# The end of a one-core transformer step, taken by stream: gates by slot, sums of squares by products with ones, the last two experts added apart

## The chip, the core and the metric

One core of a Trainium2 chip runs the whole program. TensorE (PE in the profile, its weight loads PEld) multiplies into PSUM banks; VectorE (DVE), ScalarE (ACT) and GpSimd (POOL) work elementwise; SyncE (SP) issues the transfers. The metric is the device time of one execution in microseconds (us), the median of the runs. Less is better.

## The reference, cut to what matters

Two streams of 128 tokens (prompt and sample, 256 token columns in all) go through one layer: a mixer, then a mixture of 32 experts of which each token takes four, then a final norm. Only the end bears on this change:

```python
def expert_step(acc, e):
    w_gu_e, b_gu_e, w_down_e, b_down_e, w_tok = e
    g, u = jnp.split(t @ w_gu_e + b_gu_e, 2, axis=-1)
    g = jnp.minimum(g, SWIGLU_LIMIT)
    u = jnp.clip(u, -SWIGLU_LIMIT, SWIGLU_LIMIT)
    act = (u + 1.0) * g * jax.nn.sigmoid(SWIGLU_ALPHA * g)
    out = act @ w_down_e + b_down_e
    return acc + w_tok[:, None] * out, None
...
x = x + g2 * _moe(h, lp)        # g2: one gate per channel and stream
...
y = x * rsqrt(mean(x * x) + EPS) * norm_final
```

## The kernel before, in words

The residual `xT` lies transposed: 128 partitions of channels, eight tiles (`k` 0 to 7) of 256 token columns, the first 128 of them one stream and the rest the other. Each expert's weights come in six transfers of 2 MB (four for gate and up, `w_gu`; two for down, `w_dn`) into eleven places that are used in turn (`load_unit`, line 389, issue on line 402); SP issues them in one queue, well ahead of their use.

An expert (`expert`) works on up to 64 tokens that chose it, its slots. `up` calls `expert_up`: 64 matmul records for gate and up (line 1233; each fp32 product stands as two records), in the order in which the four pieces land, then four short bias products (line 1238). `expert_act` does the activation on VectorE and ScalarE (lines 1246 to 1250): clip the gate half, tanh on ScalarE, clip the up half, two multiplications. `down` of the expert before turns the activation round (`transposed`, line 1285, copied on line 1288) and multiplies it by the down weights (line 1298); `keep_y` copies the result. Experts are added in pairs: `scatter_pair` builds the matrix that spreads slots back to tokens (lines 1257 to 1272, tile `sT`), and `add_out` (line 1313) spreads and adds into `xT` through `add_gated` (line 1177), which multiplies by the channel's gate `fin[:, s, k]`. An even expert has slots 0 to 63 in channel tiles 0 to 3 and slots 64 to 127 in tiles 4 to 7; an odd one has the other halves.

TensorE's order in an expert is written by hand (`manual_schedule`); the other engines' instructions are ordered by the scheduler. For the last expert, 31, the order is: `bias_products` (the down biases by the routing weights), down of expert 30, `scatter_pair(30)`, up of 31, its activation, and `add_out(bias, "pa", ...)`, the bias term added to `xT`. PSUM banks are named by tags: C has two, A has three, B, D and E one each.

`finale` (line 1467) then runs alone: down of expert 31; per quarter `c`, the copy of its result beside expert 30's, the spreading products (line 1480), the gated adds into `xT`, squares on ScalarE (line 1483) and the norm weight on ScalarE or GpSimd (lines 1487, 1489); GpSimd adds three squares together (line 1493); column sums by products with one column of ones (line 207); GpSimd's power for 1/sqrt on 128x2 (line 193); TensorE spreads it over the partitions (line 201); VectorE multiplies (lines 1509, 1513) and five transfers write `o_tokens` (line 1514).

Of the kernel before, what the change touches and what calls it, by code (L numbers as in the profile page):

```python
# [20 lines left out]
P = 128  # L21
# [42 lines left out]
def hybrid_step(ctx, tc, A):  # L64
# [324 lines left out]
    def load_unit(u, h):  # L389
# [11 lines left out]
        for i in range(0, k, step):  # L401
            npc_ins[0] = nc.sync.dma_start(t[:, i:i + step], src[:, i:i + step])
# [781 lines left out]
    def bias_products():  # L1184
# [8 lines left out]
        cbT = place(6 * NE % NUNIT, "cbT", 0)[:, 0:2 * P].rearrange("e (s t) -> e s t", s=2)  # L1193
# [26 lines left out]
    def expert_up(e, xg, w, banks, m, after=None, half_way=None):  # L1220
# [5 lines left out]
        for k in range(KC):  # L1226
            if half_way and k == KC // 2 - 1:
                half_way()
            with tc.issue_after(after.ins) if after else ExitStack():
                for i in range(2):  # L1230
                    for q in range(nq):
                        c0 = i * D + part[q] * wd
                        PE.matmul(banks[i][m * q:m * q + m, 0:wd], xg[:, k, :], w[k][:, c0:c0 + wd],  # L1233
                                  start=(k == 0), stop=False, skip_group_check=True)
        for i in range(2):
            for q in range(nq):
                c0 = i * D + part[q] * wd
                PE.matmul(banks[i][m * q:m * q + m, 0:wd], sel3[:, e:e + 1].to_broadcast([96, m]), b3[:, c0:c0 + wd],
                          start=False, stop=True, skip_group_check=True)
        return banks  # L1240

    def expert_act(banks, name, m, tag="gm"):
# [4 lines left out]
        S.activation(tg, gm, AF.Tanh, scale=0.851)  # L1247
        V.tensor_scalar(um, banks[1][:, 0:wd], 7.0, -7.0, op0=ALU.min, op1=ALU.max)
        V.scalar_tensor_tensor(gm, tg, 1.0, gm, op0=ALU.add, op1=ALU.mult)
        V.scalar_tensor_tensor(gm, um, 1.0, gm, op0=ALU.add, op1=ALU.mult)  # L1250
        return gm

# [55 lines left out]
    def add_out(products, name, tags="CCCC"):  # L1308

        for j in range(0, KC, 2):  # L1310
            pc = bank(tags[j // 2], f"{name}pc{j}", 3 if tags[j // 2] == "A" else 2)
# [3 lines left out]
        return ins  # L1315

# [96 lines left out]
    def up(e):  # L1413
        return expert_up(e, xgs.pop(e), w, up_banks(e, f"e{e}pgu"), CAP, last,
                         (lambda: gather_first(0, (1,)), lambda: down(0))[e] if e < 2 else None)
# [4 lines left out]
    def expert(e):  # L1420
# [13 lines left out]
        if e == NE - 1:  # L1434
            bias = bias_products()
        if e > 1:
            last = down(e - 1)
            if e % 2:
                scatter_pair(e - 1)

# [7 lines left out]
        acts[e] = (expert_act(banks, f"e{e}", CAP), w)  # L1448
# [6 lines left out]
        else:  # L1455

            add_out(bias, "pa", ("C", "C", "A", "A"))
# [9 lines left out]
    def finale():  # L1467
        down(NE - 1)
        y, py = ys[NE - 2], last_y[0]
        pss = bank("E", "pssl", 1)  # L1470
        products = pair_products(sT[NE - 2], y)
        sq = place((6 * NE + 1) % NUNIT, "sql", 0)[:, 0:2 * D].rearrange("p (k t) -> p k t", t=T)

        def finish(c):

            cs = slice(c * P, (c + 1) * P)
            keep_y(y, py, 1, cs)
            pc = bank("C", f"pcl{c}", 2)
            for i, k in enumerate((c, c + 4)):
                PE.matmul(pc[:, i * T:(i + 1) * T], *products[k], start=True, stop=True)  # L1480
            add_tiles_gated((c, c + 4), pc)
            for k in (c, c + 4):
                S.activation(sq[:, k], xT[:, k], AF.Square)
            if c < 3:
                for k in (c, c + 4):
                    if c < 2:
                        S.activation(xT[:, k], xT[:, k], AF.Copy, scale=fin[:, 2, k:k + 1])
                    else:
# [110 lines left out]
```

## Time and profile before

| | us |
|---|---|
| median of 3 runs | 1434.85 |
| lowest, highest | 1432.95, 1436.88 |
| the profiled execution | 1435.31 |
| its span | 1433.5 |

Over the span PE is busy for 1339.8 us (93%), DVE for 590.3, ACT for 335.9 and POOL for 104.2; HBM is read at 352 GB/s on the mean, and in the stretch of the experts at some 424 GB/s. [...] In a timeline row the numbers are the start in the span, the time from the first start to the last end of the merged instructions, and in brackets the idle time before them with what ended it.

### The profile page before, as it was taken

What the parts mean: (1) busy time and instruction counts of PE and PEld (TensorE: products, weight loads), DVE (VectorE), ACT (ScalarE), POOL (GpSimd) and SP (SyncE); (2) the same over time, 40 slices, a digit from 0 to 9 for tenths busy, and PEclk for the clock granted to TensorE, in tenths of its full rate; (3) what the DMA queues carried; (4) which work ended last, traced back from release to release, by engine and by line L of the source; (5) the groups of instructions that cost most, each with busy time, mean ns of one, the idle gap of its engine ahead of it and who ended that gap; (6) DMA issues with size and microseconds to landing.
All of it is one profiled execution on the core that took longest, in us unless ns stands there. A gap on an engine that the chain in (4) does not pass through costs nothing. (4 is left out here: it accounts for less than half of the span.)

```text
span 1433.5 us, 20977 instructions
## 1 busy us (share of the span) xinstructions
PE 1339.8 (93%) x8577; PEld 793.9 (55%) x8577; DVE 590.3 (41%) x1270; ACT 335.9 (23%) x631; POOL 104.2 (7%) x118
## 2 busy tenths in 40 slices
PE   7999999999999999999999899999999999898885
PEld 3988989898999643443443344344344343333332
DVE  4856879898776322132132222213213212212124
ACT  2534656575664110010000000001001000000001
POOL 1112313431002000000000000000000000000001
PEclk8999999999999999999999999999999999999997
DMA  9997566556877899999999999999999999999981
GB/s 360 294 278 203 186 231 235 215 181 224 318 284 263 333 406 424 423 426 423 423 427 424 410 423 425 424 426 423 425 424 426 424 424 425 425 425 424 426 337 35
DMA packets 83710, 506.53 MB, mean 353 GB/s; under 512 B 6866, under 2 KB 34130, under 8 KB 51410
## 3 DMA queue, kind: packets, MB, share of 16 engines
q1 hardware_dynamic: 80658, 497.71, 87.1%
q10 hardware_dynamic: 2880, 6.60, 1.3%
q8 instruction: 99, 1.62, 0.5%
q14 instruction: 73, 0.60, 0.1%
HBM read 498.26 MB, written 5.64 MB: 352 GB/s over the span
## 5 line engine op out<-in xcount | busy, mean ns | idle before, releaser
L303 DVE TENSOR_TENSOR wl<-win,wh 128x1024 fp32r<-128x1024 f32 (+1 forms) x84 | 100.7, 1211 | 36.0 <-ACT wh L302 24.7
L302 ACT CAST wh<-win 128x1024 fp32r<-128x1024 f32 (+1 forms) x84 | 84.0, 1010 | 73.4 <-PE pbc L330 19.2
L1493 POOL TENSOR_TENSOR sql<-sql 128x256 f32<-128x256 f32 x3 | 2.2, 727 | 944.9 <-PE pcl L1480 944.6
L714 POOL TENSOR_TENSOR m<-m_half,adt 128x512 fp32r<-128x512 f32 x32 | 42.5, 1347 | 87.1 <-PE pss L717 87.1
L330 PE MATMUL pxs<-hT,wh 128*128 128x256 f32 x256 | 37.5, 291 | 0.0
L330 PE MATMUL pgt<-hT,wh 128*128 128x256 f32 x256 | 36.0, 287 | 1.0 <-ACT wh L302 1.0
L330 PE MATMUL pz<-hT,wh 128*128 128x256 f32 x256 | 36.7, 288 | 0.0
L330 PE MATMUL pbc<-hT,wh 128*128 128x256 f32 x256 | 35.6, 287 | 0.0
L330 PEld LDWEIGHTS pxs<-hT,wh 128*128 128x128 f32 x256 | 32.5, 190 | 3.6 <-issue 2.8
L330 PE MATMUL pso<-yhl,wh 128*128 128x256 f32 x256 | 34.1, 284 | 0.0
L330 PEld LDWEIGHTS pgt<-hT,wh 128*128 128x128 f32 x256 | 32.4, 191 | 3.0 <-issue 1.9
L330 PEld LDWEIGHTS pz<-hT,wh 128*128 128x128 f32 x256 | 32.5, 190 | 1.5 <-issue 1.5
L330 PEld LDWEIGHTS pbc<-hT,wh 128*128 128x128 f32 x256 | 32.2, 190 | 1.9 <-issue 1.7
L330 PEld LDWEIGHTS pso<-yhl,wh 128*128 128x128 f32 x256 | 32.1, 192 | 0.0
L330 PE MATMUL pglu<-hT,wh 128*128 128x256 f32 x192 | 27.1, 292 | 0.0
L330 PEld LDWEIGHTS pglu<-hT,wh 128*128 128x128 f32 x192 | 25.1, 199 | 0.7 <-issue 0.7
L303 DVE TENSOR_TENSOR wl<-wso,wh 128x1024 fp32r<-128x1024 f32 x16 | 19.5, 1223 | 7.5 <-ACT wh L302 7.3
L697 ACT ACTIVATE gd<-gm,dtT 128x128 f32<-128x128 f32 x64 | 20.8, 415 | 4.4 <-DVE gm L688 4.3
L698 DVE SCALAR_TENSOR_TENSOR gd<-gm,dtT,gd 128x128 f32<-128x128 f32 x64 | 21.0, 377 | 1.6 <-ACT gd L697 1.2
L302 ACT CAST wh<-wso 128x1024 fp32r<-128x1024 f32 x16 | 16.7, 1046 | 14.3 <-PE pso L330 10.8
L330 PE MATMUL pwo<-mhl,wh 128*128 128x256 f32 x128 | 18.9, 290 | 0.3 <-DVE mhl L1008 0.3
L1233 PE MATMUL e26pgu<-w,xg 128*64 128x512 f32 x64 | 16.1, 654 | 3.2 <-DMA w<-in_w_gu 2.9
(1095 smaller groups left out, 2632.8 us busy)
## 6 DMA issues: line engine op xcount, KB each, us to landing
w<-in_w_gu SPq DMA_DIRECT2D x116, 2048.0 KB, 30.4
w<-in_w_down SPq DMA_DIRECT2D x57, 2048.0 KB, 26.3
win<-in_w_in_pack SPq DMA_DIRECT2D x38, 1024.0 KB, 6.5
ada<-in_w_ada SPq DMA_DIRECT2D x10, 1024.0 KB, 9.1
wso<-in_w_ssd_out SPq DMA_DIRECT2D x8, 1024.0 KB, 6.0
im<-dru SPq DMA_DIRECT2D x16, 312.0 KB, 8.5
wcf<-in_w_conf_out SPq DMA_DIRECT2D x4, 1024.0 KB, 8.8
wo<-in_w_o SPq DMA_DIRECT2D x4, 1024.0 KB, 9.7
```

Of the source, the lines that this page charges most:

```text
L302: S.copy(hi[:, ks, 0:m], w[:, ks])
L303: V.tensor_tensor(lo[:, ks, 0:m], w[:, ks], hi[:, ks, 0:m], ALU.subtract)
L330: last_wo[0] = PE.matmul(out, w[:, k, 0:n], m[:, k, :], start=first and i == 0, stop=last and i == len(order) - 1, skip_group_check=True)
L697: S.activation(gd[s][:, h, :], gm[:, 0, s, :], AF.Copy, scale=dtT[:, 0, s, c0:c0 + 1])
L698: V.scalar_tensor_tensor(gd[s][:, h, :], gm[:, 1, s, :], dtT[:, 0, s, 32 + c0:33 + c0], gd[s][:, h, :], op0=ALU.mult, op1=ALU.add)
L714: G.tensor_tensor(m4[d], m_half[:, d, None, None, :].to_broadcast([P, 2, 4, 64]), ac[d], ALU.mult)
L1233: PE.matmul(banks[i][m * q:m * q + m, 0:wd], xg[:, k, :], w[k][:, c0:c0 + wd], start=(k == 0), stop=False, skip_group_check=True)
L1493: G.tensor_tensor(sq[:, 0], sq[:, 0], sq[:, k], ALU.add)
```

## The change

It touches the last expert and what follows it, and one transfer.

- The transfer of piece 1 of expert 28 is issued as three, of 112, 7 and 9 rows.
- `expert_up` of expert 31 multiplies its last two row tiles for the gate half first, adds the gate's bias, and then does the up half. `expert_act` does its first multiplication before it clips the up half.
- Before expert 31's up products, TensorE writes the gates as rows (`gates_by_slot`: 16 transposes of a broadcast column into banks C, copied to SBUF by ScalarE in four halves).
- Expert 30's share is no longer added with expert 31's. `add_two` adds the bias term and expert 30's slots together, for four channel tiles before expert 31's up products and for the other four after its activation.
- The end: VectorE multiplies expert 31's down result by the gates, once per stream, out of PSUM; TensorE spreads it (half of the partitions for each product, 128 columns of one stream); VectorE adds `xT`; ScalarE squares; products of a 128x128 block of ones with the squares give the sums already spread over the partitions; the norm weight, the scale and the power (GpSimd, now on 128x128 for each stream) follow; four transfers write the output, by stream and half of the channels.

```diff
--- before.py
+++ after.py
@@ -399,7 +399,8 @@
         step = k // 2 if e == NE - 1 and c > 3 else k
         for i in range(0, k, step):
-            npc_ins[0] = nc.sync.dma_start(t[:, i:i + step], src[:, i:i + step])
+            for r in (slice(0, 112), slice(112, 119), slice(119, P)) if (e, c) == (28, 1) else (slice(0, P),):
+                npc_ins[0] = nc.sync.dma_start(t[r, i:i + step], src[r, i:i + step])
         return [t[:, i] for i in range(k)]
     def parts(u):
@@ -1181,7 +1182,7 @@
             for s in range(2):
                 add_gated(k, s, pc[:, i * T + s * P:i * T + (s + 1) * P])
-    def bias_products():
+    def bias_products(spare):
         b_dn = con.tile([P, D // 4], F32, name="b_dn", tag="g1_0")
         S.dma_start(b_dn, A["b_down_pack"])
@@ -1190,7 +1191,7 @@
             for s in range(2):
                 PE.matmul(pct[q * NE:(q + 1) * NE, s * P:(s + 1) * P], comb[:, s], ident, start=True, stop=True,
                           skip_group_check=True)
-        cbT = place(6 * NE % NUNIT, "cbT", 0)[:, 0:2 * P].rearrange("e (s t) -> e s t", s=2)
+        cbT = spare[:, 0:2 * P].rearrange("e (s t) -> e s t", s=2)
         V.tensor_copy(cbT, pct[:, 0:2 * P].rearrange("e (s t) -> e s t", s=2))
         rows = [slice(k // 2 * NE, (k // 2 + 1) * NE) for k in range(KC)]
         return [(b_dn[r, k % 2 * P:(k % 2 + 1) * P], cbT[r]) for k, r in enumerate(rows)]
@@ -1217,38 +1218,52 @@
     def over_banks(name, n):
         return [bank(t, f"{name}{i}", b) for i, (t, b) in enumerate((("D", 1), ("C", 2), ("C", 2), ("E", 1))[0:n])]
-    def expert_up(e, xg, w, banks, m, after=None, half_way=None):
+    def expert_up(e, xg, w, banks, m, after=None, half_way=None, gate_first=False):
         nq = P // m
         wd = D // nq
         part = (0, 1) if nq == 2 else (0, 2, 1, 3)
-        for k in range(KC):
+        def rows(k, i):
+            for q in range(nq):
+                c0 = i * D + part[q] * wd
+                PE.matmul(banks[i][m * q:m * q + m, 0:wd], xg[:, k, :], w[k][:, c0:c0 + wd],
+                          start=(k == 0), stop=False, skip_group_check=True)
+        def bias(i):
+            for q in range(nq):
+                c0 = i * D + part[q] * wd
+                PE.matmul(banks[i][m * q:m * q + m, 0:wd], sel3[:, e:e + 1].to_broadcast([96, m]), b3[:, c0:c0 + wd],
+                          start=False, stop=True, skip_group_check=True)
+        together = KC - 2 if gate_first else KC
+        for k in range(together):
             if half_way and k == KC // 2 - 1:
                 half_way()
             with tc.issue_after(after.ins) if after else ExitStack():
                 for i in range(2):
-                    for q in range(nq):
-                        c0 = i * D + part[q] * wd
-                        PE.matmul(banks[i][m * q:m * q + m, 0:wd], xg[:, k, :], w[k][:, c0:c0 + wd],
-                                  start=(k == 0), stop=False, skip_group_check=True)
+                    rows(k, i)
         for i in range(2):
-            for q in range(nq):
-                c0 = i * D + part[q] * wd
-                PE.matmul(banks[i][m * q:m * q + m, 0:wd], sel3[:, e:e + 1].to_broadcast([96, m]), b3[:, c0:c0 + wd],
-                          start=False, stop=True, skip_group_check=True)
+            for k in range(together, KC):
+                rows(k, i)
+            bias(i)
         return banks
-    def expert_act(banks, name, m, tag="gm"):
+    def expert_act(banks, name, m, tag="gm", gate_first=False):
         wd = D * m // P
         gm = sm.tile([P, wd], F32, name=name + "gm", tag=tag, bufs=1)
         tg, um = (sm.tile([P, 512], F32, name=name + n, tag=t, bufs=1)[:, 0:wd] for n, t in (("tg", "aT"), ("um", "um")))
         V.tensor_scalar(gm, banks[0][:, 0:wd], 7.0, None, op0=ALU.min)
         S.activation(tg, gm, AF.Tanh, scale=0.851)
+        if gate_first:
+            V.scalar_tensor_tensor(gm, tg, 1.0, gm, op0=ALU.add, op1=ALU.mult)
         V.tensor_scalar(um, banks[1][:, 0:wd], 7.0, -7.0, op0=ALU.min, op1=ALU.max)
-        V.scalar_tensor_tensor(gm, tg, 1.0, gm, op0=ALU.add, op1=ALU.mult)
-        V.scalar_tensor_tensor(gm, um, 1.0, gm, op0=ALU.add, op1=ALU.mult)
+        if not gate_first:
+            V.scalar_tensor_tensor(gm, tg, 1.0, gm, op0=ALU.add, op1=ALU.mult)
+        last_act_ins[0] = V.scalar_tensor_tensor(gm, um, 1.0, gm, op0=ALU.add, op1=ALU.mult)
         return gm
+    last_act_ins = [None]
     def slots_of(out, e, poss):
@@ -1305,14 +1320,25 @@
             r = slice(CAP * q, CAP * (q + 1))
             (V.tensor_copy if q else S.copy)(ys[q ^ swap][r, cols], py[r, cols])
-    def add_out(products, name, tags="CCCC"):
+    def add_out(products, name):
         for j in range(0, KC, 2):
-            pc = bank(tags[j // 2], f"{name}pc{j}", 3 if tags[j // 2] == "A" else 2)
+            pc = bank("C", f"{name}pc{j}", 2)
             for i in range(2):
                 ins = PE.matmul(pc[:, i * T:(i + 1) * T], *products[j + i], start=True, stop=True)
             add_tiles_gated((j, j + 1), pc)
         return ins
+    def add_two(one, two, c, tag, bufs, after=None):
+        pcs = [bank(tag, f"papc{c}{h}", bufs) for h in range(2)]
+        for x in (one, two):
+            for i in range(2):
+                for h in range(2):
+                    PE.matmul(pcs[h][:, i * T:(i + 1) * T], *x[c + i + 4 * h], start=x is one and i == 0, stop=x is two, skip_group_check=True)
+        with tc.issue_after(after.ins) if after else ExitStack():
+            for h in range(2):
+                add_tiles_gated((c + 4 * h, c + 4 * h + 1), pcs[h])
     def pair_products(sT, ys):
         return [(ys[k // 4][:, k % 4 * P:(k % 4 + 1) * P], sT[:, k // 4]) for k in range(KC)]
@@ -1412,7 +1438,7 @@
     def up(e):
         return expert_up(e, xgs.pop(e), w, up_banks(e, f"e{e}pgu"), CAP, last,
-                         (lambda: gather_first(0, (1,)), lambda: down(0))[e] if e < 2 else None)
+                         (lambda: gather_first(0, (1,)), lambda: down(0))[e] if e < 2 else None, e == NE - 1)
     def add_pair(e):
         return add_out(pair_products(sT[e], ys[e]), f"e{e}")
@@ -1432,11 +1458,17 @@
                 combine()
         if e == NE - 1:
-            bias = bias_products()
+            spare = place(6 * NE % NUNIT, "spare", 0)
+            bias = bias_products(spare)
         if e > 1:
             last = down(e - 1)
             if e % 2:
                 scatter_pair(e - 1)
+            if e == NE - 1:
+                gates_by_slot(spare)
+                first = [(ys[e - 1][k // 4][own(0, k // 4), k % 4 * P:(k % 4 + 1) * P], sT[e - 1][own(0, k // 4), k // 4]) for k in range(KC)]
+                add_two(bias, first, 0, "C", 2)
             load_pieces(6 * e + NUNIT)
         overflow(e, w, more)
@@ -1445,7 +1477,7 @@
             gather_first(1)
         if e == 1:
             scatter_pair(e - 1)
-        acts[e] = (expert_act(banks, f"e{e}", CAP), w)
+        acts[e] = (expert_act(banks, f"e{e}", CAP, gate_first=e == NE - 1), w)
         if e % 2 == 0:
             if e:
@@ -1454,7 +1486,24 @@
             gather_slots(e + 1)
         else:
-            add_out(bias, "pa", ("C", "C", "A", "A"))
+            add_two(bias, first, 2, "A", 3, last_act_ins[0])
+    def own(i, h):
+        return slice(CAP, P) if i ^ h else slice(0, CAP)
+    gslot = []
+    def gates_by_slot(spare):
+        for s in range(2):
+            t = spare[:, 512 + 512 * s:1024 + 512 * s]
+            for h in range(2):
+                pt = bank("C", f"pgs{s}{h}", 2)
+                for k in range(4):
+                    PE.transpose(pt[:, k * P:(k + 1) * P], fin[:, s, 4 * h + k:4 * h + k + 1].to_broadcast([P, P]), ident)
+                S.copy(t[own(1, h)], pt[own(1, h)])
+            gslot.append(t)
     w = last = mores = None
     last_y = []
@@ -1466,52 +1515,48 @@
     def finale():
         down(NE - 1)
-        y, py = ys[NE - 2], last_y[0]
-        pss = bank("E", "pssl", 1)
...
-        for k in (0, 2, 6, 3, 7):
-        rf = rstd_of(pss[:, 0:2], 1.0 / D, EPS, "rf")
-        bcast_rows(rbf, rf)
...
+        py = last_y[0]
+        sl = sT[NE - 2]
+        t = place((6 * NE + 1) % NUNIT, "fin1", 0)
+        yg = [t[:, 512 * s:512 * s + 512] for s in range(2)]
+        xs, sq = {}, {}
+        places = (t[:, 2 * D:], place((6 * NE + 2) % NUNIT, "fin2", 0))
+        for s in range(2):
+            for h in range(2):
+                xs[s, h], sq[s, h] = (places[s][:, (2 * i + h) * 512:(2 * i + h + 1) * 512].rearrange("p (k t) -> p k t", t=P) for i in range(2))
+        for s in range(2):
+            V.tensor_tensor(yg[s], py, gslot[s], ALU.mult)
+        pcs = {}
+        for s in range(2):
+            pc = [bank("CA"[s], f"pcl{s}{h}", 3 if s else 2) for h in range(2)]
+            for k in range(4):
+                for h in range(2):
+                    r = own(1, h)
+                    PE.matmul(pc[h][:, k * P:(k + 1) * P], yg[s][r, k * P:(k + 1) * P], sl[r, h, s], start=True, stop=True,
+                              skip_group_check=True)
+            for h in range(2):
+                pcs[s, h] = pc[h].rearrange("p (k t) -> p k t", t=P)
+        ss = bank("E", "ssl", 1)
+        for s in range(2):
+            for h in range(2):
+                V.tensor_tensor(xs[s, h], pcs[s, h], xT[:, 4 * h:4 * h + 4, s * P:(s + 1) * P], ALU.add)
+                S.activation(sq[s, h], xs[s, h], AF.Square)
+        for s in range(2):
+            for h in range(2):
+                for k in range(4):
+                    PE.matmul(ss[:, s * P:(s + 1) * P], one.to_broadcast([P, P]), sq[s, h][:, k],
+                              start=(h == 0 and k == 0), stop=(h == 1 and k == 3), skip_group_check=True)
+        for s in range(2):
+            for h in range(2):
+                V.tensor_tensor(xs[s, h], xs[s, h], fin[:, 2, 4 * h:4 * h + 4].unsqueeze(2).to_broadcast([P, 4, P]), ALU.mult)
+            v = yg[0][:, s * P:(s + 1) * P]
+            V.tensor_scalar(v, ss[:, s * P:(s + 1) * P], 1.0 / D, EPS, op0=ALU.mult, op1=ALU.add)
+            G.tensor_tensor(v, v, mhalf[:, 0:1].to_broadcast([P, P]), ALU.pow)
+            for h in range(2):
+                V.tensor_tensor(xs[s, h], xs[s, h], v.unsqueeze(1).to_broadcast([P, 4, P]), ALU.mult)
+                nc.sync.dma_start(A["o_tokens"][512 * h:512 * h + 512, s * P:(s + 1) * P].rearrange("(k p) t -> p k t", p=P), xs[s, h])
     with tc.manual_schedule(engines={mybir.EngineType.PE}):
         finale()
```

## Rows read from the trace of the kernel before

**Rows 1.** The windows view, last expert to last down products; its columns head it.

```profile
core 0: us, PE busy (x) PEld busy (x) DVE busy (x) ACT busy (x) POOL busy (x), PEclk, DMA share, GB/s
...
1396.00:1400.00 4.00, 3.73 (x20) 1.29 (x20) 0.00 (x0) 0.00 (x0) 0.00 (x0) 1.00 0.06 27
1400.00:1404.00 4.00, 1.46 (x20) 0.76 (x16) 3.81 (x11) 0.63 (x1) 0.00 (x0) 1.00 0.06 27
1404.00:1408.00 4.00, 1.85 (x6) 1.03 (x8) 2.89 (x10) 0.59 (x1) 0.00 (x0) 0.50 0.02 10
1408.00:1412.00 4.00, 4.00 (x14) 1.20 (x12) 0.00 (x0) 0.00 (x0) 0.00 (x0) 0.64 0.00 0
```

**Rows 2.** The chain that ended last: start us, length us, what.

```profile
1396.27 3.65 PE e31pgu L1233 x16
...
1401.47 1.11 DVE xT L1177 x4
...
1403.18 1.55 DVE xT L1177 x6
...
1407.25 8.88 PE e31py L1298 x32
...
1429.44 0.39 DVE xT L1509
```

**Rows 3.** Timeline, TensorE and ScalarE around the last expert's gate and up products.

```profile
1383.23 0.66 PE L1269 MATMUL pst<-ident,sg 128*128 128x128 f32 x4
...
1383.92 0.59 ACT L1272 COPY sT<-pst 128x512 f32<-128x512 f32 x1
...
1384.04 1.94 PE L1233 MATMUL e31pgu<-w_0a,xg 128*64 128x512 f32 x8
...
1391.39 3.65 PE L1233 MATMUL e31pgu<-w,xg 128*64 128x512 f32 x16 [0.27 <-DMA w<-in_w_gu]
...
1396.27 3.65 PE L1233 MATMUL e31pgu<-w,xg 128*64 128x512 f32 x16 [1.23 <-DMA w<-in_w_gu]
...
1399.76 0.60 PE L1238 MATMUL e31pgu<-b,sel 96*64 96x512 bf16 x4
```

**Rows 4.** Timeline, TensorE groups that price the new and moved products.

```profile
1351.99 7.09 PE L1233 MATMUL e30pgu<-w,xg 128*64 128x512 f32 x32 [0.29 <-PEq L1343]
...
1369.81 1.99 PE L1313 MATMUL e28pc<-sT,y 128*128 128x256 f32 x8
...
1374.83 0.71 PE L1285 MATMUL e30pat<-ident,e30gm 128*128 128x128 f32 x4
...
1376.21 7.09 PE L1298 MATMUL e30py<-w,e30aT 128*64 128x512 f32 x32 [0.68 <-ACT e30aT L1288]
...
1400.29 1.17 PE L1313 MATMUL papc<-cbT,b_dn 32*128 32x256 f32 x16
```

**Rows 5.** Timeline, first steps of the last expert's activation.

```profile
1400.18 0.69 DVE L1246 TENSOR_SCALAR e31gm<-e31pgu 128x512 f32<-128x512 f32 x1 [15.53 <-PE e31pgu L1238]
...
1400.79 0.68 DVE L1248 TENSOR_SCALAR e31um<-e31pgu 128x512 f32<-128x512 f32 x1
...
1400.97 0.63 ACT L1247 ACTIVATE e31tg<-e31gm 128x512 f32<-128x512 f32 x1 [16.46 <-DVE e31gm L1246]
```

**Rows 6.** Prices for the new end: timeline, then groups by line and form.

```profile
1422.57 2.70 PE L207 MATMUL pssl<-one,sql 128*128 128x1 f32 x20 [0.71 <-POOL sql L1493]
...
L854 DVE TENSOR_TENSOR modr<-modr,pm 128x512 f32<-128x512 f32 x6 | 4.1, 684 | 1.1 <-PE pm L226 1.0
...
L767 ACT ACTIVATE ysq<-y 128x512 f32<-128x512 f32 x8 | 5.0, 625 | 3.1 <-DVE y L765 3.1
```

**Rows 7.** GpSimd's groups by line and form: busy us, mean ns, idle before.

```profile
L734 POOL TENSOR_TENSOR le<-L,dtT 128x4 f32<-128x4 f32 x16 | 6.3, 418 | 10.1 <-ACT L L721 10.1
...
L1493 POOL TENSOR_TENSOR sql<-sql 128x256 f32<-128x256 f32 x3 | 2.2, 727 | 944.9 <-PE pcl L1480 944.6 <-ACT sql L1483 0.3
...
L193 POOL TENSOR_TENSOR rf<-rfv,mhalf 128x2 f32<-128x2 f32 x1 | 0.7, 719 | 1.2 <-DVE rfv L191 1.2
```

More of the change, by code (lines that the diff above doesn't have):

```diff
@@ L1468, in finale @@
         down(NE - 1)
-        y, py = ys[NE - 2], last_y[0]
-        pss = bank("E", "pssl", 1)
[L1471 to L1488, printed above, removed]
-                        G.tensor_scalar(xT[:, k], xT[:, k], fin[:, 2, k:k + 1], None, op0=ALU.mult)
@@ L1491, in add_squares @@
-        def add_squares(*ks):
-            for k in ks:
-                G.tensor_tensor(sq[:, 0], sq[:, 0], sq[:, k], ALU.add)
-        finish(0)
-        add_squares(4)
-        finish(1)
-        add_squares(1, 5)
-        finish(2)
-        finish(3)
-        for k in (0, 2, 6, 3, 7):
-            col_sums(pss, sq[:, k], k, k == KC - 1)
-        rf = rstd_of(pss[:, 0:2], 1.0 / D, EPS, "rf")
-        rbf = bank("E", "rbf", 1)
-        bcast_rows(rbf, rf)
-        for ks in ((0,), (1, 2), (3, 4), (5, 6), (7,)):
-            sl = slice(ks[0], ks[-1] + 1)
-            if 3 in ks or 7 in ks:
-                V.scalar_tensor_tensor(xT[:, ks[0]], xT[:, ks[0]], fin[:, 2, ks[0]:ks[0] + 1], rbf[:, 0:T], op0=ALU.mult, op1=ALU.mult)
-                ks = ks[1:]
-            if ks:
-                x = xT[:, ks[0]:ks[-1] + 1]
-                V.tensor_tensor(x, x, rbf[:, None, 0:T].to_broadcast([P, len(ks), T]), ALU.mult)
-            nc.sync.dma_start(A["o_tokens"][sl.start * P:sl.stop * P, :].rearrange("(k p) t -> p k t", p=P), xT[:, sl])
+        py = last_y[0]
```

## The prediction

> **What bounds the kernel now.** [...] Then the chain: it is transfers until 1396.27, when the last piece of expert 31's gate and up weights lands, and compute from there to the end of VectorE at 1429.83 [rows 2]. So 37.2 us lie between that landing and the end of the span (1433.50), and every step of the change lies in or just ahead of them. Third, the timeline around expert 31: its up products begin at 1384.04 and wait 0.27 us for the third piece and 1.23 us for the fourth [rows 3]. TensorE has therefore 1.5 us to spare before the landing, no more. Last, the groups that price the parts [rows 4 to 7].
>
> The profiled execution took 1435.31 us (span 1433.50, 1.81 around it), 0.46 over the median of 1434.85. I add up against the profile and take the difference off the median. A difference under 0.3%, 4.3 us, can't be told from none.
>
> **Ahead of expert 31.** TensorE's order is written by hand, so the 16 gate transposes and the first `add_two` stand between the scatter's transposes (1383.23 to 1383.89) and the up products (1384.04) [rows 3]. Transposes cost 0.66 us for four [rows 3]; but they go through the two C banks, and ScalarE must empty each before it is used again. ScalarE is free at 1384.51, after `sT` [rows 3]; four copies of that width at 0.59 end at about 1386.9, and then the products have both banks. They are 16 records of 256 columns. Eight of full height take 1.99 us, while 16 in four row groups took 1.17 [rows 4]. Here two row groups can run at once, so I take half of 3.98, 2.0 us. The up products start at about 1389.1, 5.1 us later than now. They now set the pace: 64 records at 7.09 per 32 [rows 4] are 14.2 us, and the bias adds 0.44, the stretch from 1399.92, the end of the last piece's products, to 1400.36 [rows 3]. Up ends at 1403.7 instead of 1400.36: **3.4 us lost**. If the transposes find gaps earlier in TensorE's stream, this loss goes to nothing (a rival below); if the products don't overlap it is 2.0 more.
>
> **The activation.** Now it runs from 1400.18 [rows 5] to 1405.34 (adds until 1404.73, then the last multiplication, 0.61), and 2.66 us of it are adds into `xT` that VectorE does in between [rows 2]. These go behind it (`issue_after`). The gate half ends half a piece (1.83) and half the bias (0.22) before the up half, at 1401.7. By the present distances (0.79 us from clip to tanh, 0.63 tanh, 0.61 between VectorE's starts [rows 5]) tanh ends at 1403.1, the first multiplication at 1403.8, the clip of the up half at 1404.5 and the last multiplication at 1405.1. But the second `add_two` is queued on TensorE ahead of the turn of the activation: another 2.0 us, 1403.7 to 1405.7. So TensorE, not VectorE, sets the turn's start, 0.4 us later than the 1405.34 at which the activation ends now, and splitting the halves buys only that the lost 3.4 us are made good. The eight adds of that second half run beside the down products.
>
> **The clock.** TensorE then has no long gap: up, `add_two`, turn. I take expert 30's rows, at full clock, for turn and down: 1.38 us from turn to down, 7.09 us for down [rows 4], against 8.88 for expert 31 now [rows 2]. Down starts at 1407.1 and ends at 1414.2, against 1416.13: **1.9 us gained**, nearly all of it from the clock. If the clock falls all the same, this gain is gone (bound: 0).
>
> **The new end**, from the end of down products, T. Two multiplications out of PSUM (0.684 each [rows 6], 0.61 apart): first done at T+0.7. The first stream's 16 records of 128 columns, two at a time: 1.0 us and 0.2 to land, T+2.05. Four adds 0.61 apart end at T+4.6. Squares follow by 0.63 each [rows 6], the first done at T+3.4, the last at T+5.2. The products with ones, 32 records at 2.70/20 = 0.135 [rows 6], run from T+3.4 to T+7.75, so they set the pace; the four norm-weight multiplications lie beside them. VectorE's step out of the sums' bank takes 0.28 (as an add of 128x128, 1.11 for four [rows 2]). Both streams share that bank, so I let it wait for the last product; if it need not, only the first stream gains, up to 1.4 us at the end. T+8.15.
>
> Then GpSimd's power, twice, on 128x128. The trace has it only on 128x2: 0.719 us [rows 7]. Other two-input work there costs 0.418 for 4 columns and 0.727 for 256, so 0.0012 us a column [rows 7]. Low bound: the power's columns cost as much, 0.719 + 0.15 = 0.87. High bound: all it costs over 0.418 is per column, 0.30/2 = 0.15 us, and 128 columns take 19.6 us. These ends are far apart. I take 0.95, near the low one, since the plain rows hardly rise with the columns, but 128x2 can't tell a start-up cost from a column's cost. The first power ends at T+9.1, the second at T+10.1; four multiplications by it from T+9.2, 0.61 apart, end at T+11.7. From VectorE's end to the span's end it is 3.67 us now [rows 2]; I keep that. T+15.4, against 17.4 now: **2.0 us gained**.
>
> [...]
>
> **The split transfer.** One 16 KB row at the 27 GB/s of the trailing engine [rows 1] is 0.6 us. The split can move a row or two of the trailing engine either way, and SP issues two more transfers. With TensorE 3 us behind the landing, neither shows: nothing, and 0.6 us either way where TensorE waits for the landing.
>
> [...] No row here shows which engine trails, so the sign stays open.
>
> **Sum:** 1.9 + 2.0 = 3.9 us; the span ends at 1429.6, and 1434.85 - 3.9 = 1430.95, **1431.0 us**.
>
> **The rivals.**
> - *TensorE is not delayed ahead of expert 31.* For it: its stream idles for 0.68 us ahead of expert 30's down products [rows 4], and the gates depend on nothing late. Against: the order by hand. Up then ends at 1400.36, the second `add_two` at 1402.4, down at 1410.8: 3.4 us more, **1427.6 us**.
> - *The power costs by the column.* The end is then T+13.2 plus twice the power; both multiplications of the last stream and the tail follow it. It is no gain from 3.05 us for a power, and 4.3 us slower than before from 5.2. At the high bound of 19.6, the end is T+52.4 and the time **1468 us**. For it: 0.30 us over plain work for two columns, the only row there is. Against: nothing in this trace has more than two.
> - *The work is only moved*: the half-height products don't overlap (2.0 us at each of two places) or the power is 2 to 3 us. The gain is used up: **1434 to 1435 us**.
>
> **How the numbers follow.** The forecast has 0.50, with a range of its own of 1428 to 1433; a little under half of it, 0.23, passes the 4.3 us. TensorE undelayed: 0.18, all of it faster. Work only moved: 0.17, no difference. Power by the column: 0.15, of which 0.14 passes 4.3 us on the slow side. That gives 0.41 faster, 0.45 within 0.3%, 0.14 slower. For 8 in 10 the range takes in the undelayed case with 1.6 us more (the first stream's early power, the split), and on the other side a power of about 4.5 us: 1426 to 1437.
>
> **What would show it.** Expert 31's first up product near 1389 and no wait for its fourth piece (right), or at 1384 to 1386 with a wait (the first rival). Granted clock of 1.00 through its down products, and 7.1 us for them. The power's two rows on 128x128: near 0.95 us, or several. From the end of down to the span's end: 15.4 us. The prediction is wrong if the power takes over 3 us, or if up ends before 1402.

## The result and the profile after

The changed kernel takes 1488.38 us (median; 1487.18 to 1489.88) against 1435.87 for the kernel before on the same chip: 1.0367 times the time before, 95% interval 1.0344 to 1.0391. That is 52.5 us slower, where 3.9 us faster was forecast. The profiled execution has a span of 1487.4 us.

The page of the changed kernel shows two places where time is lost. Here are lines of its second part, which cuts the span into 40 slices of 37.2 us:

```profile
POOL 1112324321020000000000000000000000000028
...
DMA  9896475566978899999999999999999999999701
GB/s 368 291 264 211 175 248 205 213 220 210 333 238 356 348 425 425 424 426 422 426 424 417 422 424 423 426 424 423 426 425 424 425 424 425 267 414 424 316 8 28
```

GpSimd is busy in the last two slices, in which no weights move any more. And in slice 34, counted from 0, the transfers fall from 425 to 267 GB/s while their engines stay busy nine tenths or more. The page's chain, by engine, and its costliest group name the first place:

```profile
POOLq 3%; PE 2%; DVE 0%; ACT 0%; DVEq 0%; issue 0%; POOL 0%
...
L1556 POOL TENSOR_TENSOR fin<-fin,mhalf 128x128 f32<-128x128 f32 x2 | 41.4, 20720 | 965.5 <-DVE fin L1555 965.5
```

**One power over 128x128 takes 20.72 us**, against 0.719 over 128x2 before [rows 7]. There are two, one behind the other, and the multiplication of the last stream waits for the second. The windows of the changed kernel (PEclk is TensorE's granted clock, then the transfers' share and rate) show the second place:

```profile
core 0: us, PE busy (x) PEld busy (x) DVE busy (x) ACT busy (x) POOL busy (x), PEclk, DMA share, GB/s
...
1265.00:1270.00 5.00, 4.78 (x16) 1.52 (x18) 0.42 (x1) 0.00 (x0) 0.00 (x0) 0.66 1.01 415
1270.00:1275.00 5.00, 5.00 (x26) 1.67 (x24) 0.00 (x0) 0.00 (x0) 0.00 (x0) 1.00 1.06 223
1275.00:1280.00 5.00, 2.41 (x12) 0.58 (x8) 0.00 (x0) 0.00 (x0) 0.00 (x0) 1.00 0.99 200
...
1290.00:1295.00 5.00, 3.43 (x11) 1.26 (x13) 0.00 (x0) 0.00 (x0) 0.00 (x0) 0.75 0.98 210
1295.00:1300.00 5.00, 2.73 (x10) 0.69 (x8) 0.00 (x0) 0.00 (x0) 0.00 (x0) 0.84 0.97 339
1300.00:1305.00 5.00, 4.71 (x18) 1.41 (x16) 0.00 (x0) 0.41 (x1) 0.00 (x0) 0.73 1.03 426
1305.00:1310.00 5.00, 3.49 (x16) 0.93 (x14) 0.86 (x2) 0.17 (x1) 0.00 (x0) 1.00 0.99 375
...
1426.00:1430.00 4.00, 4.00 (x20) 1.33 (x20) 0.68 (x3) 0.00 (x0) 0.00 (x0) 1.00 0.02 4
```

For some 27 us from 1270 on, **the weights come at half rate with a transfer share of 1.0**: the transfer engines are not short of work, the packets take twice their time (those of 16 KB have a median of 1.24 us between 1270 and 1297 and of 0.61 us there in the kernel before). The kernel before has 419 to 431 GB/s in the same stretch:

```profile
1275.00:1280.00 5.00, 5.00 (x28) 1.76 (x25) 0.35 (x1) 0.00 (x0) 0.00 (x0) 1.00 1.01 426
```

The split piece is the one whose first part is issued at 1259.5, and what follows is 18.5 us late: expert 30's scatter transposes begin at 1401.73 (below), 18.50 us behind 1383.23 [rows 3].

Half rate for 27 us is only some 13.7 us of lost transfers (27 x (425 - 210)/425). The rest is lost by the queue that is last. The rate dips once more after 1305, with the share still near 1.0. By the landings in the trace, the first share of the second half of expert 31's piece 0 arrives 12.5 us later than in the kernel before (1373.1 against 1360.6), and its last share 18.5 us later (1399.0 against 1380.5). A product waits for the last share (in the kernel before the last share of expert 31's fourth piece lands at 1396.23, and its products begin at 1396.27 [rows 2]), so the loss is what the slowest queue loses.

The rest is in the timeline of the changed kernel, expert 31 and the new end. To compare a time up to the down products with the kernel before, take 18.50 off:

```profile
1401.73 0.66 PE L1284 MATMUL pst<-ident,sg 128*128 128x128 f32 x4
...
1402.23 1.04 PE L1504 MATMUL pgs<-ident,fin 128*128 128x128 f32 x8
...
1403.67 1.25 PE L1504 MATMUL pgs<-ident,fin 128*128 128x128 f32 x8 [0.41 <-ACT spare L1505]
1404.99 1.73 PE L1338 MATMUL papc<-spare,b_dn 32*128 32x256 f32 x8
1406.65 1.13 PE L1338 MATMUL papc<-sT,y 64*128 64x256 f32 x8
...
1407.97 1.94 PE L1230 MATMUL e31pgu<-w_0a,xg 128*64 128x512 f32 x8 [0.19 <-PEq L1369]
...
1421.94 0.42 PE L1236 MATMUL e31pgu<-b,sel 96*64 96x512 bf16 x2
...
1424.42 0.75 PE L1300 MATMUL e31pat<-ident,e31gm 128*128 128x128 f32 x4
...
1425.84 7.09 PE L1313 MATMUL e31py<-w,e31aT 128*64 128x512 f32 x32 [0.68 <-ACT e31aT L1303]
1432.97 1.29 DVE L1529 TENSOR_TENSOR fin<-e31py,spare 128x512 f32<-128x512 f32 x2 [6.30 <-PE e31py L1313]
...
1436.32 4.04 PE L1549 MATMUL ssl<-fin,one 128*128 128x128 f32 x32 [0.54 <-ACT fin L1544]
...
1440.40 0.49 DVE L1555 TENSOR_SCALAR fin<-ssl 128x128 f32<-128x128 f32 x2 [0.41 <-PE ssl L1549]
1440.82 41.41 POOL L1556 TENSOR_TENSOR fin<-fin,mhalf 128x128 f32<-128x128 f32 x2 [965.53 <-DVE fin L1555]
...
1482.26 1.29 DVE L1558 TENSOR_TENSOR fin<-fin,fin 128x512 f32<-128x512 f32 x2 [19.20 <-POOL fin L1556]
```

Up to the step ahead of the power at 1440.40, all of it but the 18.50 us lies within some 0.7 us of where the forecast put it. The first of the two powers ends at about 1461.5, the second at 1482.2, and the span ends 5.2 us after that.

### The profile page after: what moved, and what is told of

Read it like the earlier page. It is cut to its first block, busy times and chain, and to the rows that moved or that the text cites. A ratio compares the mean times of both kernels' runs of the same rounds, so it can differ in the third digit from the quotient of the medians.

```text
span 1487.4 us, 21074 instructions
## 1 busy us (share of the span) xinstructions
PE 1346.0 (90%) x8635; PEld 797.4 (54%) x8635; DVE 591.5 (40%) x1259; ACT 334.9 (23%) x623; POOL 140.8 (9%) x114
## 5 line engine op out<-in xcount | busy, mean ns | idle before, releaser
L1556 POOL TENSOR_TENSOR fin<-fin,mhalf 128x128 f32<-128x128 f32 x2 | 41.4, 20720 | 965.5 <-DVE fin L1555 965.5
L302 ACT CAST wh<-win 128x1024 fp32r<-128x1024 f32 (+1 forms) x84 | 83.9, 1009 | 73.4 <-PE pbc L330 19.2
L1230 PE MATMUL e28pgu<-w,xg 128*64 128x512 f32 x64 | 17.1, 694 | 5.8 <-DMA w<-in_w_gu 5.5
```

The lines of the kernel that those rows point to most:

```text
L302: S.copy(hi[:, ks, 0:m], w[:, ks])
L1556: G.tensor_tensor(v, v, mhalf[:, 0:1].to_broadcast([P, P]), ALU.pow)
```

## The experiments

Two theories stood first: that the split transfer costs the 18.5 us, and that the power's columns cost the 40. Their rivals were that the new work of the other engines delays the loads, and that something around the power makes it slow. Each loss was taken away alone, the split was put into the kernel before alone, and both were taken away.

**The plain piece.** The changed kernel without the split:

```diff
-            for r in (slice(0, 112), slice(112, 119), slice(119, P)) if (e, c) == (28, 1) else (slice(0, P),):
-                npc_ins[0] = nc.sync.dma_start(t[r, i:i + step], src[r, i:i + step])
+            npc_ins[0] = nc.sync.dma_start(t[:, i:i + step], src[:, i:i + step])
```

> The changed kernel with piece 1 of expert 28 loaded by one plain 128-row transfer again; all else as changed. Theory (the split transfer runs the weight stream at half rate for 27 us and costs 18.5 us): the total falls by 18.5 to about 1470 us, ratio to the kernel before 1.024; expert 30's third up piece begins at about 1360.9 again instead of 1379.4, and no stretch of 1270 to 1300 shows less than 400 GB/s. Rival (the loads are late because of the new work on the other engines - gate tiles, earlier adds, places held longer - and the split has nothing to do with it): 1488 us, ratio 1.037, the 190 to 223 GB/s stretch stays.

Measured: 1470.97 us, 1.0246 [1.0229, 1.0263], 17.4 less than the changed kernel. Windows of this kernel:

```profile
1275.00:1280.00 5.00, 5.00 (x33) 2.87 (x30) 1.82 (x3) 0.63 (x1) 0.00 (x0) 1.00 0.99 419
```

The slow stretch is gone, though all the other new work is there.

**The split alone.** The kernel before with the two lines of the split, and nothing else.

> The kernel before, with only the row split (112, 7 and 9 rows) of piece 1 of expert 28 added. Theory (split costs 18.5 us by itself): 1435.9 + 18.5 = 1454 us, ratio 1.013, the same stretch of about 200 GB/s from 1270 on. Rival (the split is free and the new work delays the loads): 1435 to 1436, ratio 1.000.

Measured: 1454.81 us, 1.0123 [1.0106, 1.0140], 19.2 more than before. Windows:

```profile
1275.00:1280.00 5.00, 1.75 (x10) 0.50 (x8) 0.00 (x0) 0.00 (x0) 0.00 (x0) 1.00 1.02 210
1280.00:1285.00 5.00, 5.00 (x30) 2.29 (x27) 1.29 (x2) 0.51 (x1) 0.00 (x0) 1.00 1.05 213
```

The rival (1435 to 1436) falls: the split does it without any of the new work.

**The narrow power.** The changed kernel, split and all, with the sums in columns:

```diff
-                    PE.matmul(ss[:, s * P:(s + 1) * P], one.to_broadcast([P, P]), sq[s, h][:, k],
+                    PE.matmul(ss[:, s:s + 1], sq[s, h][:, k], one,
...
+        rf = rstd_of(ss[:, 0:2], 1.0 / D, EPS, "rf")
+        rbf = bank("E", "rbf", 1)
+        bcast_rows(rbf, rf)
...
-            v = yg[0][:, s * P:(s + 1) * P]
-            V.tensor_scalar(v, ss[:, s * P:(s + 1) * P], 1.0 / D, EPS, op0=ALU.mult, op1=ALU.add)
-            G.tensor_tensor(v, v, mhalf[:, 0:1].to_broadcast([P, P]), ALU.pow)
+            v = rbf[:, s * P:(s + 1) * P]
```

> The changed kernel with the sums of squares taken as 128x2 columns, the power on 128x2 and the result spread by two transposes, as the kernel before did; the split stays. Theory (GpSimd's power costs 0.16 us for each column, so 2 x 20.7 us of the end are the power): the end shrinks by about 2 x 20 = 40 us, gives back 1 to 2 us for the two transposes and the extra hop, 1448 to 1451 us, ratio 1.009 to 1.011, with one power of 0.7 us. Rival (the power is slow because of something around it, such as its broadcast exponent or the library being loaded, and stays slow when narrow): one slow power of up to 20 us remains, 1467 to 1470 us.

Measured: 1451.85 us, 1.0107 [1.0090, 1.0124], 36.5 less than the changed kernel. Its power, among its groups:

```profile
L193 POOL TENSOR_TENSOR rf<-rfv,mhalf 128x2 f32<-128x2 f32 x1 | 0.7, 688 | 965.5 <-DVE rfv L191 965.5
```

Same engine, same operation, same place in the end, one thirtieth of the time, so the rival of a power that stays slow falls. The time is 0.9 us above the theory's range. Two things differ between the two powers, the columns and an exponent that is broadcast in the wide one only; the power over 32 columns, below, tells them apart.

**Both mended.** The edits of the plain piece and of the narrow power together.

> The changed kernel with the plain load and the narrow power. Theory (the two losses are separate and add, and the rest of the change is worth what the forecast gave it, 3 to 5 us, before the narrow path's hop of 1 to 2 us): 1488.4 - 18.5 - 39 = 1431 us, 1429 to 1433, ratio 0.995 to 0.998. Rival (the two losses share a cause or hide each other): not the sum, but 1440 us or more.

Measured: 1433.69 us, 0.9985 [0.9975, 0.9994], 1.9 less than before, 0.7 above the theory's range and far from the rival's 1440. The two losses are separate and add: 1488.4 less 17.4 and 36.5 is 1434.5. What is left of the gain is small, and the narrow path takes part of it. Its timeline:

```profile
1421.03 4.99 PE L1548 MATMUL ssl<-one,fin 128*128 128x1 f32 x32 [0.54 <-ACT fin L1543]
...
1426.37 0.69 POOL L193 TENSOR_TENSOR rf<-rfv,mhalf 128x2 f32<-128x2 f32 x1 [948.07 <-DVE rfv L191]
1427.11 0.69 PE L201 MATMUL rbf<-ident,rf 128*128 128x128 f32 x2 [1.08 <-POOL rf L193]
1427.84 2.48 DVE L1558 TENSOR_TENSOR fin<-fin,rbf 128x512 f32<-128x512 f32 x4 [1.61 <-PE rbf L201]
```

The sums in columns take 4.99 us where the wide ones take 4.04, and from the power's end to the first multiplication it is 0.8 us for the transposes. From the end of the down products to the end of the span it is 17.4 us here, the same as before the change.

**What of the split is slow?** Three theories. A: the queues of a transfer each take their share of its rows, so that in a transfer split by rows a queue works on rows that in the plain transfers belong to another, and while both kinds are under way they get in each other's way; by A, even and odd rows in two transfers leave each queue the rows of a plain one. B: each further transfer takes one of the eight semaphores on which SP waits (in the trace of the kernel before eight count all landings), and the queues that are ahead run dry. C: transfers of 7 and 9 rows are bad by themselves (in the trace of the changed kernel they land in 7 and 9 shares, a plain piece in 16). Four splits in the kernel before tell them apart; the first three change only the list of row slices of the split, the fourth only the expert.

```diff
+            for r in (slice(0, 64), slice(64, P)) if (e, c) == (28, 1) else (slice(0, P),):          # halves in blocks
+            for r in (slice(0, P, 2), slice(1, P, 2)) if (e, c) == (28, 1) else (slice(0, P),):      # halves interleaved
+            for r in (slice(0, 112), slice(112, P)) if (e, c) == (28, 1) else (slice(0, P),):        # 112 and 16
+            for r in (slice(0, 112), slice(112, 119), slice(119, P)) if (e, c) == (8, 1) else (slice(0, P),):  # early
```

> The kernel before, with piece 1 of expert 28 in two transfers, rows 0 to 63 and rows 64 to 127. Theory A (the sixteen queues share a transfer's rows in blocks, so that in another split each queue reads and writes other rows than in the plain transfers that the queues ahead or behind are still on; while both kinds run, every packet takes twice its time): slow stretch of 20 to 30 us and a loss of 10 to 20 us, 1446 to 1456. Theory B (the loss is one of number: each further transfer takes one of the eight semaphores on which SP waits, so the queues ahead run dry): one further transfer instead of two, about half the loss, 1444 to 1446, with idle queues and no packet slower. Theory C (transfers of 7 and 9 rows alone do it, since few queues serve them): 1436.

> [...] Theory A: no slow stretch, 1435 to 1437. Theory B: as the halves in blocks, 1444 to 1446. Theory C: 1436, as the halves in blocks.

> The kernel before, with piece 1 of expert 28 in rows 0 to 111 and rows 112 to 127, both numbers that sixteen queues share evenly (7 rows and 1 row each). Theory A: the slow stretch and nearly the whole loss, 1450 to 1456. Theory B: one further transfer, half the loss, 1444 to 1446. Theory C: no transfer of 7 or 9 rows is left, 1436.

> The kernel before, with the change's own split (112, 7 and 9 rows) on piece 1 of expert 8 instead of expert 28: there the last queue is some 4 us behind the first, against 18 us at expert 28. Theory A: the two kinds of transfer meet for 4 + 9 us instead of 18 + 9, the slow stretch is 13 us instead of 27 and the loss some 9 us, 1443 to 1446. Theory B: with little spread the first queue never runs dry, 1436. Theory C: as at expert 28, 1454.

Measured: halves in blocks 1453.07 us, 1.0125 [1.0093, 1.0157]; halves interleaved 1436.20, 1.0004 [0.9985, 1.0024]; 112 and 16 rows 1452.52, 1.0122 [1.0092, 1.0151]; the early split 1446.28, 1.0085 [1.0051, 1.0120]; the kernel before beside them 1434.72. The windows, first of the halves in blocks, then of the interleaved ones:

```profile
1275.00:1280.00 5.00, 3.94 (x20) 1.23 (x18) 0.00 (x0) 0.00 (x0) 0.00 (x0) 1.00 1.01 216
```

```profile
1275.00:1280.00 5.00, 5.00 (x26) 1.73 (x24) 0.00 (x0) 0.00 (x0) 0.00 (x0) 1.00 1.01 429
```

Two transfers of 64 rows each in both cases, with the same bytes in the same packets; one loses 18.4 us, the other nothing that can be measured. So number (B) isn't the cause, and the share of 1.01 at 216 GB/s says so too: no queue is dry in that stretch. Nor is it the few rows (C): with 112 and 16, both multiples of sixteen, 17.8 us are lost. Windows of the early split:

```profile
675.00:680.00 5.00, 4.71 (x24) 1.68 (x22) 1.22 (x3) 1.16 (x2) 0.00 (x0) 1.00 1.10 262
680.00:685.00 5.00, 5.00 (x26) 1.80 (x24) 0.00 (x0) 0.00 (x0) 0.00 (x0) 1.00 1.06 203
685.00:690.00 5.00, 5.00 (x26) 1.75 (x24) 0.00 (x0) 0.00 (x0) 0.00 (x0) 1.00 0.92 170
690.00:695.00 5.00, 5.00 (x43) 4.28 (x40) 3.27 (x5) 0.69 (x2) 0.00 (x0) 1.00 0.95 298
```

Its slow stretch is some 16 us instead of 27, its loss 11.6 instead of 19.2. What differs is how far apart the queues are: by the landings in the trace, the first and the last share of one piece arrive at 651.2 and 656.1 us here, 4.9 apart, and in the kernel before at 1252.6 and 1270.6, 18.0 apart, for a piece issued ahead of the one that the change splits. The two kinds of transfer meet for longer where the last queue is further behind. A gave a loss of 9; the interval of the 11.6 goes from 7 to 17, so the direction is shown and the exact size is not. The profile doesn't name the queue of a packet, so that the queues meet is inferred from these lengths.

**Which side?** A transfer reads rows in memory and writes partitions. Two pieces were loaded in halves with a different split on each side (the kernel before; expert 18's piece is one that the kernel loads in two parts of half the width, so it comes in four transfers of 64 rows of 8 KB, where expert 28's comes in two of 16 KB; these two pieces' rows land on other partitions than they should, so the time is that of the loads and of unchanged work on them):

```diff
+            half, every = [slice(0, 64), slice(64, P)], [slice(0, P, 2), slice(1, P, 2)]
+            moved = {(18, 1): (every, half), (28, 1): (half, every)}.get((e, c), ([slice(0, P)],) * 2)
+            for to, of in zip(*moved):
+                npc_ins[0] = nc.sync.dma_start(t[to, i:i + step], src[of, i:i + step])
```

> The kernel before, with two pieces each loaded as two transfers of 64 rows, so that the two sides of a transfer are split differently: piece 1 of expert 18 (loaded around 965 us) is read from memory in halves and written to even and odd partitions, piece 1 of expert 28 (around 1265 us) is read as even and odd rows and written to partitions 0 to 63 and 64 to 127. The rows of these two pieces land on other partitions than they should, so this is a measurement of the loads alone. Theory A, on the written side (queues that write other partitions than usual meet the others there): slow stretch of 20 to 30 us from 1270 on only, 1452 to 1455. Theory A, on the read side (they meet in memory): slow stretch of some 17 us around 970 only, 1445 to 1450. Either side is enough: both stretches, 1462 to 1468.

Measured: 1452.81 us, 1.0119 [1.0099, 1.0139]. Its windows at expert 18, written to even and odd partitions, and at expert 28, written in blocks:

```profile
970.00:975.00 5.00, 3.80 (x20) 2.12 (x22) 4.07 (x15) 0.59 (x1) 0.00 (x0) 1.00 1.00 426
975.00:980.00 5.00, 5.00 (x26) 1.62 (x23) 0.00 (x0) 0.10 (x1) 0.00 (x0) 1.00 0.98 413
...
1275.00:1280.00 5.00, 0.22 (x2) 0.22 (x4) 0.00 (x0) 0.00 (x0) 0.00 (x0) 0.76 0.98 210
1280.00:1285.00 5.00, 5.00 (x14) 1.40 (x14) 0.00 (x0) 0.00 (x0) 0.00 (x0) 0.55 1.03 210
```

Partitions in halves bring the slow stretch and the whole loss, though the memory rows are read in the even and odd order that cost nothing above. Memory rows in halves bring none, at expert 18, where the queues are some 9 us apart. It is the written side.

**The power's price.** The changed kernel with the plain piece, the power over 32 of the 128 columns; the other 96 go without it.

```diff
-            G.tensor_tensor(v, v, mhalf[:, 0:1].to_broadcast([P, P]), ALU.pow)
+            G.tensor_tensor(v[:, 0:32], v[:, 0:32], mhalf[:, 0:1].to_broadcast([P, 32]), ALU.pow)
```

> The changed kernel with the plain load, and with the power taken over 32 of the 128 columns only; the other 96 columns are left without it. Theory (a power costs GpSimd 0.39 us and 0.159 us for each column, from 0.71 us at 2 columns and 20.72 at 128): 5.5 us for each of the two, 1470 less 2 x 15.2 = 1440 us. Rival (a fixed price once the operand is broadcast or the tile is wide): near 20 us still, 1469; rival (a price by partitions and columns in blocks, not a line): 3 us or less, or 10 us and more.

Measured: 1441.05 us, in one run, against the theory's 1440, and in its groups:

```profile
L1555 POOL TENSOR_TENSOR fin<-fin,mhalf 128x32 f32<-128x32 f32 x2 | 10.8, 5413 | 945.9 <-DVE fin L1554 945.9
```

5.41 us at 32 columns, 20.72 at 128, 0.69 at 2: (20.72 - 5.41)/96 = 0.159 us a column, (5.41 - 0.69)/30 = 0.157. It is a line, and the power at 2 columns, whose exponent isn't broadcast, lies on it too: the columns make the price.

**Without GpSimd.** The changed kernel with the plain piece, and a square root on ScalarE and a reciprocal on VectorE in the power's place; then the same with the first pair of adds behind expert 31's transposes.

```diff
+        S.activation(wk.tile([P, 2], F32, name="warm", tag="rv", bufs=2)[:, 0:1], ident[:, 0:1], AF.Sqrt)
...
-            G.tensor_tensor(v, v, mhalf[:, 0:1].to_broadcast([P, P]), ALU.pow)
+            S.activation(v, v, AF.Sqrt)
+            V.reciprocal(v, v)
```

> The changed kernel with the plain load, and with a square root on ScalarE and a reciprocal on VectorE over 128x128 in place of GpSimd's power (one square root of a 128x1 column ahead of the end, so that a load of the function's table lies beside expert 31's down products). Theory (the rest of the end is as fast as the forecast said, down's end + 15): from the last square to the first of the last multiplications 2.5 us instead of the 4.3 us of the narrow power, 1431 to 1433 us, ratio 0.997. Rival (the reciprocal or a second load of the table takes the power's place): each costs 1.3 us or more on the chain that ends last, 1434 to 1437.

Measured: 1434.49 us, 0.9992 [0.9980, 1.0003], in the rival's range and above the theory's. Its timeline:

```profile
1389.35 1.94 PE L1229 MATMUL e31pgu<-w_0a,xg 128*64 128x512 f32 x8 [0.18 <-PEq L1368]
...
1407.22 7.09 PE L1312 MATMUL e31py<-w,e31aT 128*64 128x512 f32 x32 [0.68 <-ACT e31aT L1302]
...
1419.01 1.23 ACT L1544 ACTIVATE fin<-fin 128x512 f32<-128x512 f32 x2 [0.76 <-DVE fin L1543]
...
1420.25 1.28 ACT L1556 ACT_TABLE_LOAD   x1
1421.78 0.49 DVE L1555 TENSOR_SCALAR fin<-ssl 128x128 f32<-128x128 f32 x2 [0.40 <-PE ssl L1549]
1422.11 0.57 ACT L1556 ACTIVATE fin<-fin 128x128 f32<-128x128 f32 x2 [0.57 <-DVE fin L1555]
1422.45 1.76 DVE L1557 RECIPROCAL fin<-fin 128x128 f32<-128x128 f32 x2 [0.18 <-ACT fin L1556]
1424.13 1.22 DVE L1559 TENSOR_TENSOR fin<-fin 128x512 f32<-128x512 f32 x2
```

The table's load isn't ahead of the end as meant (the square root that was to bring it ran at 475.8 us, long before the last tanh), but it is done at 1421.53, before the input of the square roots is there, and costs nothing. The two reciprocals take 1.76 us, and both come ahead of the first multiplication: from the last square (1420.24) to there it is 3.9 us, not 2.5.

```diff
-        last = down_products(transposed(gm, f"e{e}", CAP), w, py, CAP, e % 2)
+        at = transposed(gm, f"e{e}", CAP)
+        if e == NE - 1:
+            add_two(*late_adds, 0, "C", 2)
+        last = down_products(at, w, py, CAP, e % 2)
...
-                add_two(bias, first, 0, "C", 2)
...
+            late_adds.extend((bias, first))
             add_two(bias, first, 2, "A", 3, last_act_ins[0])
...
+    late_adds = []
...
```

> As the square-root kernel, and the first pair of adds (the bias and expert 30 for the first half of the columns), which stood ahead of expert 31's up products, goes between expert 31's transposes and its down products. Theory (from 1369 us on TensorE is the bound, so 2.9 us ahead of the up products are lost there, while 0.7 us of the gap before the down products are free): the up products start 2.9 us earlier, the down products 0.5 to 1 us, 1430 to 1432 us. Rival (the up products then wait for expert 31's weights, as they did before the change by 1.5 us): same time as the square-root kernel, or up to 1.6 us more.

Measured: 1431.60 us, 0.9965 [0.9951, 0.9980]: 4.4 us less than before, a small gain that its interval tells from none. Its timeline:

```profile
1386.56 1.94 PE L1229 MATMUL e31pgu<-w_0a,xg 128*64 128x512 f32 x8
...
1404.75 1.13 PE L1337 MATMUL papc<-sT,y 64*128 64x256 f32 x8
1405.82 7.09 PE L1312 MATMUL e31py<-w,e31aT 128*64 128x512 f32 x32
```

Expert 31's up products begin 2.8 us earlier than in the square-root kernel (1389.35) and wait 0.3 us for weights in all, and the down products begin 1.4 us earlier (1405.82 against 1407.22). About half of the 1.4 is the 0.7 us of gap ahead of the down products, which the adds now fill; the rest is that they take 2.1 us there, where ahead of the up products they took 2.8, waiting for ScalarE to empty a bank (its copies end at 1386.92, 0.55 us after the adds' first product). The profiled spans differ by the same 1.4 us (1431.2 and 1429.8); the medians differ by 2.9, and no row shows the rest.

## Why the prediction was wrong

Two terms of the sum failed, and they make the whole difference: with a power at 20.72 instead of 0.95 us, twice, and the split at the 17.4 to 19.2 us of the two experiments instead of nothing, the forecast's 1431.0 becomes 1488 to 1490. Measured: 1488.4.

- **The power (new end), mis-sized: 0.95 us forecast, 20.72 measured.** The two bounds follow from their rows, and the high one, 19.6, was almost the price. The step that failed is the choice between them. It went by the plain rows, which hardly rise with the columns [rows 7], but these are another operation. The one row of the power itself cost 0.30 us over the plain one for two columns, and read as a price by the column that is 0.15; the runs show 0.157 to 0.159. The rival by the column, 1468 us, is what the plain piece gave within 3 us (1470.97). It had a chance of 0.15 on the only row that there was of the operation itself; that row deserved more, and the range left its bound out.
- **The split transfer, costed at nothing: 17.4 to 19.2 us.** The step asked which queue carries a row more or less, and not what the queues that are ahead do while the split piece is written. The bound of 0.6 us either way came from the price of one row on a quiet last queue, at 27 GB/s and a share of 0.06, one sixteenth [rows 1]; that the split moves a row or two of that queue was the author's estimate, and no trace here names the queue of a row. In the stretch in which the piece is loaded, some 165 us before the end of the kernel before, all queues are at work (a share of 1.01 to 1.02 from 1265 to 1280), and no row there was read. The 7- and 9-row transfers weren't what mattered: the loss is as large without one (17.8 us with 112 and 16 rows).
- **TensorE ahead of expert 31: right.** The up products begin at 1407.97 - 18.50 = 1389.47 (forecast 1389.1) and end at 1403.86 (1403.7). Two small misses nearly cancel in it: the adds begin 0.4 us earlier than forecast, and the first `add_two` takes 3.0 us to the first up product where some 2.2 were taken, because its second bank is free only when ScalarE's last copy ends, at 1405.54 (its first eight records take 1.73 us, where the second pair's take 1.13). The last kernel shows that those adds really cost there: moved, the up products began 2.8 us earlier.
- **The activation: right.** TensorE's second `add_two`, not VectorE, precedes the transposes: they begin at 1405.92 after the shift (1405.7).
- **The clock: right.** The granted clock is 1.00 in the down products, where the kernel before had 0.50 and 0.64 up to 1412 [rows 1]; they take 7.09 us, against 8.88 [rows 2], and end at 1414.4 after the shift (1414.2).
- **The new end without the power: right.** VectorE's two steps out of the sums' bank lie at T+7.5 to T+8.0 (T+8.15), T being the end of the down products at 1432.93. The end of the span is T+54.5; less 2 x 19.77 us, what the two powers took over 0.95, it is T+15.0 (T+15.4). That is an estimate: in no run does the wide power take 0.95 us.
- **The sum.** Its parts hold, but the gain without the two losses could be had only with some other way to 1/sqrt: 17.4 us of end with the narrow power and 16.9 with the square root instead of 15. That fits the two mended kernels, which stand at 0.9985 and 0.9992.

## What to carry to other kernels

Where an operation stands in the trace at one size only, take its price over a plain operation of the same engine as a price by the element until a run shows otherwise, and don't use it at sixty-four times the width; a result that is the same in every partition was cheaper here as two columns and two transposes (17.4 us of end) than as a power over the whole width (54.5). Split a transfer in a busy stream of like transfers only so that each part is spread over the partitions as the whole ones are (even and odd rows, 1.0004 here, not blocks, 1.0125), and judge it from the stretch in which it is loaded, by its last queue. Work on the engine that sets the pace is free only in its gaps: the same adds cost 1.4 us more ahead of the up products than behind the transposes, half of it for a gap that they fill there.

## What the runs showed of the hardware

- GpSimd's power costs some 0.4 us and 0.157 to 0.159 us a column: 0.69 us on 128x2, 5.41 on 128x32, 20.72 on 128x128, where other two-input work takes 0.727 on 128x256 [rows 7].
- A piece of 2 MB written in two or three blocks of partitions instead of one, in a stream of plain pieces, brings the whole stream from 425 to about 210 GB/s for some 27 us, with the transfer share at 1.0; early, with the queues 5 us apart instead of 18, for some 16 us. The queue that is last loses more than the first (18.5 us against 12.5). Even and odd partitions cost nothing that can be measured (1.0004, 0.9985 to 1.0024), and memory rows read in halves bring no slow stretch (413 to 426 GB/s).
- Why the written partitions matter is not shown: no trace here tells what holds the packets up. The rate of the split piece alone doesn't give the loss: 2 MB at the 216 GB/s of the halves in blocks instead of 425 would be some 4.8 us late (an estimate from those two rates), and 18.4 us are lost.
- Two reciprocals on VectorE take 1.76 us on 128x128 where two multiply-and-adds take 0.49, and a load of ScalarE's function table takes 1.28 us.
